# Two-tile sums and products of a decoder trunk moved from GpSimd to VectorE

## The chip, the core and the metric

The kernel runs on one core of one Trainium2 chip. The core has five engines with an instruction queue each: TensorE (PE in the profile; its weight loads are PEld), VectorE (DVE), ScalarE (ACT), GpSimd (POOL) and SyncE (SP, which here only issues DMAs). Each engine works its queue in order; semaphores tie the queues together. The metric is the device time of one execution in microseconds (us); lower is better.

## The reference

A decoder trunk of two layers over 1024 tokens of width 1024, in float32. Layer 0 has a mixer of differential attention (4 heads, two softmax maps each) beside causal pooling (4 groups of 128 channels, trailing means over 2, 4, 8 and 16 tokens minus the token itself); layer 1 has a gated short convolution. After the mixer each layer has cross-attention into 256 memory tokens and a squared-ReLU MLP of width 4096. Each sub-layer is preceded by an RMSNorm and followed by a residual addition.

```python
def even_mixer(h, w_in, w_out, ...):
    ...
    o = diff_attention(q1, q2, k1, k2, v, lam, bias_dist)
    o = rms_norm(o, subln_g) * (1.0 - lambda_init)
    y = multi_scale_pool(u, pool_w, pool_scale)      # windows 2, 4, 8, 16
    return jnp.concatenate([o, y], axis=-1) @ w_out

def odd_mixer(h, w_in, conv_w, w_out):
    z = c_gate * x_part                              # three parts of h @ w_in
    y = conv3(z, conv_w)                             # causal, 3 taps
    return (b_gate * y) @ w_out

def reference(x, mem, ...):
    h = x
    for l in range(2):
        h = h + (even_mixer if l % 2 == 0 else odd_mixer)(rms_norm(h, ...), ...)
        h = h + cross_attention(rms_norm(h, ...), mem_n, wq, wkv, wo)
        a = jax.nn.relu(rms_norm(h, ...) @ w1)
        h = h + (a * a) @ w2
    return rms_norm(h, final_norm_g)
```

## The kernel before

Activations lie channel-major: a tile is 128 channels by 1024 tokens, and an activation of width 1024 is eight such tiles. Every matrix product is computed three times in a fast format of TensorE: `cut` splits a float32 tile into a high part (written by ACT, L72 or L75) and a low part (the rest, a subtraction on DVE, L73 or L76), and PE adds high by high, low by high and high by low in PSUM.

**Weights.** `order` lists all weight blocks in the sequence of their use. `w_load` starts their DMAs on SP into raw buffers `wr` (four of them), `w_cut` cuts one block into `wh` and `wl` (two each). The products with wq, w1 and w2 use a scheme of seven block products instead of eight (`split_gemm`, matmuls on L277). Its weights come in pair units of two raws `a` and `b` (72 units). A unit gives four weight blocks: `a`, the sum tile `wt`, the changed `a`, and half of `b`. Four sums of 128x512 make them: L149 and L150 write the two halves of `wt`, L152 and L153 change `a` after it has been cut. L135 to L139 are the same for the last unit. Before, these sums run on POOL.

**Products.** `split_gemm` runs its seven steps over three PSUM banks (`_x` and the two halves of `_yz`). After each step `out` evacuates a bank with raised priority: L1021 (ACT), L1023 and L1025 (DVE) in the MLP's first product (tiles `m0a`, `m1a`), L1095 (DVE) in its second (`m0b`, `m1b`), L912 in the query product of the cross-attention (`c0q`, `c1q`). A step that writes a bank waits until the bank has been evacuated.

**MLP.** `up(p)` runs 16 rounds per layer; behind each, `squares` applies scale, ReLU and square (L1010 on DVE, L1011 on ACT), `combine` forms operand sums on DVE (L259 to L262), and `store` sends the round's result to DRAM. The second product has 4 chunks of 4 steps; `fetch` and `ready` bring the stored tiles back and cut them (`m1A_...`), for the next chunk while this one runs.

**Norms.** `Norm.add` adds the squares of a tile: ACT squares it into `sq` (L323) and POOL adds it into `acc` (L324; in four places with `last=True` DVE does it). `stage1` sums over channels with PE transposes (L332) and a DVE reduction (L333), and takes the power on POOL (L336); `stage2` spreads the result with PE again (L345).

**Attention and pooling.** In the first 400 us products for the four heads and four pooling groups fill PE between the steps of the softmax chains (L579 and L580 on DVE, L581 on ACT, L590, L591, L593 on DVE, transposes L612 and products L628 on PE). `fill_u(g)` computes the channels `u` of a pooling group and then a chain of doubling sums: g+1 levels of shift-and-add, a correction of the first columns, scaling, and the subtraction of `u`. Before, all of it stands on POOL right behind `u` (L518 to L526), and the cut of the result follows as `window` some program steps later: `soon(n, fn)` runs `fn` after `n` further steps.

**Order.** The loop over `k` at the start (cuts of the input `x` and of the first weights `w0p`, squares of `x`, and the first products `q0ps`, `k0ps` on L415) stands under a manual schedule: each engine takes its instructions in the order in which they are written. The rest is placed by the language's scheduler by priority and its own estimate of durations, so that instructions moved to another engine also move their neighbours. The convolution, `conv_mixer`, multiplies twice on POOL per tile (L1148, L1155).

Of the kernel before, what the change touches and what calls it, by code (L numbers as in the profile page):

```python
# [13 lines left out]
AF = mybir.ActivationFunctionType  # L14
# [26 lines left out]
def hybrid_trunk(ctx: ExitStack, tc: tile.TileContext, xT, memT, vecs, lams, rel, onehot, negrow, invcnt,  # L41
# [21 lines left out]
    def f32(t):  # L63
        return t.bitcast(F32)
# [53 lines left out]
    def w_cut():  # L118
        u, g = state["unit"], state["group"]
        if u >= len(order):  # L120
            return
        shape = list(order[u][0])
        raw = raws[u]
        hi = sb.tile(shape, F32R, tag="wh", bufs=2, name=f"wh{u}_{g}")
        lo = sb.tile(shape, F32R, tag="wl", bufs=2, name=f"wl{u}_{g}")
        done = False
        if len(raw) == 1:
            cut(hi, lo, raw[0])
            done = True
        else:  # L130
            a, b = raw[0], raw[1]
            if g == 0 and u in tails:
                t = sb.tile(shape, F32, tag="wt", bufs=1, name=f"wt{u}")
                raw.append(t)
                nc.gpsimd.tensor_add(t[:, 4:], b[:, :4], b[:, 4:])  # L135
                nc.gpsimd.tensor_sub(t[:, :4], b[:, :4], a[:, :4])
                nc.gpsimd.tensor_sub(b[:, :4], a[:, :4], t[:, 4:])
                cut(hi, lo, a)
                nc.gpsimd.tensor_add(a[:, 4:], a[:, 4:], b[:, :4])  # L139
            elif u in tails:  # L140
                if g < 3:
                    cut(hi, lo, raw[g])
                else:
                    cut(hi[:, :4], lo[:, :4], a[:, 4:])
                    done = True
            elif g == 0:
                t = sb.tile(shape, F32, tag="wt", bufs=1, name=f"wt{u}")
                raw.append(t)
                nc.gpsimd.tensor_add(t[:, 4:], b[:, :4], b[:, 4:])  # L149
                nc.gpsimd.tensor_sub(t[:, :4], a[:, :4], t[:, 4:])  # L150
                cut(hi, lo, a)
                nc.gpsimd.tensor_sub(a[:, :4], b[:, :4], a[:, :4])  # L152
                nc.gpsimd.tensor_add(a[:, 4:], a[:, 4:], t[:, :4])  # L153
            elif g == 1:
                cut(hi, lo, raw[2])
            elif g == 2:
                cut(hi, lo, a)
            else:
                cut(hi[:, :4], lo[:, :4], b[:, 4:])
                done = True  # L160
        cuts.append((hi, lo))
        state["group"] += 1
# [144 lines left out]
    class Norm:  # L307
# [7 lines left out]

        def add(self, src, h=None, last=False):
            cs = slice(0, S) if h is None else half(h)
# [3 lines left out]
            else:  # L321
                acc, sq = self.acc[None], slot(f"{self.name}_sq")
                nc.scalar.activation(sq[:, cs], src, AF.Square)  # L323
                (nc.vector if last else nc.gpsimd).tensor_add(acc[:, cs], acc[:, cs], sq[:, cs])  # L324

# [179 lines left out]
    def fill_u(g):  # L505
# [7 lines left out]
        yield from gemm_halves(X, nm, ev)  # L513
        cur = u
        for lvl in range(g + 1):
            sh = 1 << lvl
            nxt = slot(f"{nm}_s{lvl}")
            nc.gpsimd.tensor_add(nxt[:, sh:], cur[:, sh:], cur[:, : S - sh])  # L518
            nc.gpsimd.tensor_copy(nxt[:, :sh], cur[:, :sh])
            cur = nxt  # L520
        pc = {}

        nc.gpsimd.tensor_mul(cur[:, : w - 1], cur[:, : w - 1], icnt[:, g, : w - 1])
        pl = slot(f"{nm}_p")
        nc.gpsimd.tensor_scalar(cur, cur, 1.0 / w, 1.0, op0=ALU.mult, op1=ALU.mult)
        nc.gpsimd.tensor_sub(pl, cur, u)  # L526

        def window():
            pc[0], pc[1] = pair(f"{nm}_p")
            nc.scalar.activation(pc[0], pl, AF.Copy)  # L530
            nc.gpsimd.tensor_sub(pc[1], pl, f32(pc[0]))
            soon(8, tail)
# [9 lines left out]

        soon(10 + 7 * (g + 1), window)

# [285 lines left out]
    def residual(act, g_col, name, split=False):  # L830
# [4 lines left out]
        for n in range(KT):  # L835
# [10 lines left out]
            if split and n == KT - 1:  # L846
                w, ps = w_next(), psg(f"{name}_{n}")
                for h in range(2):
# [152 lines left out]
    def mlp(l, X, nrm, g_next, name):  # L1001
# [78 lines left out]
        for c in range(4):  # L1080
            for p in range(KT // 2):
# [53 lines left out]
    def conv_mixer(X, nrm, g_next, name):  # L1135
        hooks = with_norm(nrm)
        Y = Halves()
        for j in range(KT):
# [122 lines left out]
```

## Time and profile before

| | |
|---|---|
| time, median of 3 runs | 2588.26 us (2587.04 to 2589.97) |
| the profiled execution | 2590.47 us, of which 2588.7 us are the span of its instructions |
| granted TensorE clock, mean | 0.993 |
| busy: PE, DVE, ACT, POOL | 2513.6, 1739.8, 1069.1, 729.2 us |
| instructions on DVE and POOL in the profile | 1972, 439 |

The span is the time from the first to the last instruction of the profiled execution, and its rows are in microseconds from its start. A row of the timeline gives start, duration, engine, line, operation, output and inputs; in square brackets stands how long the engine had waited and for whom. Neighbouring rows of one form are merged with a count. The row's duration is longer than the distance to the next start, since neighbours overlap a little at their ends.

### The profile page before, as it was taken

How to read it: one execution, taken by the hardware profiler on the slowest of the kernel's cores; microseconds unless marked ns; L12 is line 12 of the kernel's file. 1: busy time of each engine (PE TensorE's matmuls, PEld its weight loads, DVE VectorE, ACT ScalarE, POOL GpSimd, SP SyncE). 2: the span in 40 equal slices, each digit the busy share in tenths (PEclk: the TensorE clock that was granted, in tenths of full speed). 3: DMA queues.
4: the chain of work that ended last, by engine and by line, in shares of the span. 5: the costliest groups of instructions: out<-in, count | busy, mean ns of one | idle time of the engine just before them, and what ended most of it. 6: DMA issues, size and time to landing. Idle time of an engine off the chain costs nothing. (4 is left out here: it accounts for less than half of the span.)

```text
span 2588.7 us, 30102 instructions
## 1 busy us (share of the span) xinstructions
PE 2513.6 (97%) x11522; PEld 2053.3 (79%) x11522; DVE 1739.8 (67%) x1972; ACT 1069.1 (41%) x1503; POOL 729.2 (28%) x439
## 2 busy tenths in 40 slices
PE   7999999999999999999999999999999999999997
PEld 5777778888878888777888888878887888777786
DVE  7767764756577778877773333575567777877875
ACT  4554564445443344433342111344544334433432
POOL 3222200330224334323352111231033334322334
PEclk9999999999999999999999999999999999999999
DMA  5101146221324436776732111322133444776752
GB/s 172 33 25 42 57 155 211 106 76 64 123 94 142 170 136 224 280 272 246 258 139 73 49 49 50 138 79 92 49 122 114 156 157 159 264 272 242 267 204 92
DMA packets 108432, 365.91 MB, mean 141 GB/s; under 512 B 12416, under 2 KB 14848, under 8 KB 108288
## 3 DMA queue, kind: packets, MB, share of 16 engines
q1 hardware_dynamic: 74880, 252.82, 28.8%
q10 hardware_dynamic: 33408, 111.16, 11.3%
q8 instruction: 91, 1.49, 0.2%
q14 instruction: 53, 0.43, 0.1%
HBM read 249.91 MB, written 114.03 MB: 141 GB/s over the span
## 5 line engine op out<-in xcount | busy, mean ns | idle before, releaser
L72 ACT ACTIVATE wh<-wr 128x1024 fp32r<-128x1024 f32 (+1 forms) x318 | 305.9, 962 | 806.8 <-PE m0b_yz L277 147.2
L73 DVE TENSOR_TENSOR wl<-wr,wh 128x1024 fp32r<-128x1024 f32 (+1 forms) x318 | 365.9, 1151 | 109.9 <-ACT wh L72 109.7
L152 POOL TENSOR_TENSOR wr<-wr,wr 128x512 f32<-128x512 f32 x71 | 104.4, 1470 | 762.8 <-DVE wl L73 758.6
L73 DVE TENSOR_TENSOR wl<-wt,wh 128x1024 fp32r<-128x1024 f32 x72 | 148.4, 2062 | 7.3 <-ACT wh L72 7.1
L153 POOL TENSOR_TENSOR wr<-wr,wt 128x512 f32<-128x512 f32 x71 | 142.0, 2000 | 0.0
L150 POOL TENSOR_TENSOR wt<-wr,wt 128x512 f32<-128x512 f32 x71 | 135.5, 1909 | 5.3
L149 POOL TENSOR_TENSOR wt<-wr 128x512 f32<-128x512 f32 x71 | 101.4, 1428 | 122.7 <-issue 75.0
L72 ACT ACTIVATE wh<-wt 128x1024 fp32r<-128x1024 f32 x72 | 75.9, 1055 | 62.7 <-PE m1b_x L277 18.7
L1148 POOL TENSOR_TENSOR cv_z<-cv_z,cv_cg 128x1024 f32<-128x1024 f32 x8 | 26.2, 3275 | 175.4 <-DVE cv_z L1147 175.4
L201 PE MATMUL X<-Y,wh 128*128 128x512 f32 x256 | 69.8, 390 | 0.0
L581 ACT ACTIVATE s_p<-s,s_negm 128x128 f32<-128x128 f32 (+7 forms) x64 | 47.2, 739 | 29.1 <-DVE s_negm L580 26.1
L201 PEld LDWEIGHTS X<-Y,wh 128*128 128x128 f32 x256 | 48.0, 188 | 10.2 <-DVE X1h L851 0.3
L1010 DVE SCALAR_TENSOR_TENSOR m0a_r<-m0a_r,c0o_rbc 128x1024 f32<-128x1024 f32 x32 | 52.8, 1656 | 0.9
L1010 DVE SCALAR_TENSOR_TENSOR m1a_r<-m1a_r,c1o_rbc 128x1024 f32<-128x1024 f32 x32 | 52.8, 1656 | 0.9
L1011 ACT ACTIVATE m1a_r<-m1a_r 128x1024 f32<-128x1024 f32 x32 | 34.0, 1062 | 43.3 <-DVE m1a_r L1010 43.3
L1011 ACT ACTIVATE m0a_r<-m0a_r 128x1024 f32<-128x1024 f32 x32 | 34.0, 1062 | 43.3 <-DVE m0a_r L1010 43.3
L324 POOL TENSOR_TENSOR c1o_acc<-c1o_acc,c1o_sq 128x1024 f32<-128x1024 f32 x6 | 15.5, 2588 | 119.5 <-ACT c1o_sq L323 119.5
L324 POOL TENSOR_TENSOR c0o_acc<-c0o_acc,c0o_sq 128x1024 f32<-128x1024 f32 x6 | 15.5, 2589 | 118.6 <-ACT c0o_sq L323 118.6
L1025 DVE TENSOR_TENSOR m1a_r<-m1a_r,m1a_yz 128x512 f32<-128x512 f32 x32 | 22.0, 686 | 36.9 <-PE m1a_yz L277 36.4
L1025 DVE TENSOR_TENSOR m0a_r<-m0a_r,m0a_yz 128x512 f32<-128x512 f32 x32 | 22.0, 686 | 36.9 <-PE m0a_yz L277 36.4
L580 DVE TENSOR_REDUCE s_negm<-s 128x1 f32<-128x128 f32 (+7 forms) x64 | 46.4, 748 | 0.2
L324 POOL TENSOR_TENSOR X_acc<-X_acc,X_sq 128x1024 f32<-128x1024 f32 x6 | 15.5, 2587 | 92.7 <-ACT X_sq L323 92.7
(2695 smaller groups left out, 7999.2 us busy)
## 6 DMA issues: line engine op xcount, KB each, us to landing
wr<-in_w_dram SPq DMA_DIRECT2D x128, 512.0 KB, 3.9
m0f<-m0a_d SPq DMA_DIRECT2D x48, 512.0 KB, 6.1
m1f<-m1a_d SPq DMA_DIRECT2D x48, 512.0 KB, 5.9
wr<-in_wkv_dram SPq DMA_DIRECT2D x32, 512.0 KB, 3.6
m0a_d<-m0a_r ACTq DMA_DIRECT2D x32, 512.0 KB, 2.8
m1a_d<-m1a_r ACTq DMA_DIRECT2D x32, 512.0 KB, 2.9
wr<-in_conv_in_dram SPq DMA_DIRECT2D x24, 512.0 KB, 3.6
wr<-in_wq_dram SPq DMA_DIRECT2D x16, 512.0 KB, 3.7
```

The lines of the kernel that those rows point to most:

```text
L72: nc.scalar.activation(hi, src, AF.Copy)
L73: nc.vector.tensor_sub(lo, src, f32(hi))
L149: nc.gpsimd.tensor_add(t[:, 4:], b[:, :4], b[:, 4:])
L150: nc.gpsimd.tensor_sub(t[:, :4], a[:, :4], t[:, 4:])
L152: nc.gpsimd.tensor_sub(a[:, :4], b[:, :4], a[:, :4])
L153: nc.gpsimd.tensor_add(a[:, 4:], a[:, 4:], t[:, :4])
L201: nc.tensor.matmul(ps, wt[:, k, :], act.part(k, i, h), start=(k == 0 and wt is hi and i == 0), stop=(k == ks - 1 and wt is lo))
L324: (nc.vector if last else nc.gpsimd).tensor_add(acc[:, cs], acc[:, cs], sq[:, cs])
L580: nc.vector.tensor_reduce(s["negm"][:, m : m + 1], ps[:, :L], axis=AX.X, op=ALU.max, negate=True)
L581: nc.scalar.activation(s["pr"][m][:, :L], ps[:, :L], AF.Exp, bias=s["negm"][:, m : m + 1], accum_out=s["den"][:, m : m + 1])
L1010: nc.vector.scalar_tensor_tensor(v, v, 0.0, b(), op0=ALU.max, op1=ALU.mult)
L1011: nc.scalar.activation(t, t, AF.Square)
```

## The change

All two-tile sums and products of the weight units, the norms, the pooling and the convolution are issued on DVE instead of POOL. `Norm.add` loses its argument `last`. The pooling is also rewritten: the levels of the doubling sum are no longer issued in one piece behind `u`, but dealt over later program steps by `soon(4 + 6 * lvl, ...)`; ACT copies the first columns of a level (L521 after), the correction stays a product (L526), scaling and subtraction become one instruction (L527), and the result's low part is cut by `cut`. On POOL remain the powers (L336, L723), the zero fills (L617), the products of the last norm (L1173) and set-up: 61 instructions instead of 427. DVE has 2301 instead of 1932.

```diff
@@ w_cut: weight sums of a pair unit (the last unit likewise) @@
             elif g == 0:
...
-                nc.gpsimd.tensor_add(t[:, 4:], b[:, :4], b[:, 4:])
-                nc.gpsimd.tensor_sub(t[:, :4], a[:, :4], t[:, 4:])
+                nc.vector.tensor_add(t[:, 4:], b[:, :4], b[:, 4:])
+                nc.vector.tensor_sub(t[:, :4], a[:, :4], t[:, 4:])
                 cut(hi, lo, a)
-                nc.gpsimd.tensor_sub(a[:, :4], b[:, :4], a[:, :4])
-                nc.gpsimd.tensor_add(a[:, 4:], a[:, 4:], t[:, :4])
+                nc.vector.tensor_sub(a[:, :4], b[:, :4], a[:, :4])
+                nc.vector.tensor_add(a[:, 4:], a[:, 4:], t[:, :4])
@@ Norm.add @@
-                (nc.vector if last else nc.gpsimd).tensor_add(acc[:, cs], acc[:, cs], sq[:, cs])
+                nc.vector.tensor_add(acc[:, cs], acc[:, cs], sq[:, cs])
@@ fill_u @@
-        cur = u
-        for lvl in range(g + 1):
+        cur = {0: u}
+        pc = {}
+
+        def level(lvl):
             sh = 1 << lvl
             nxt = slot(f"{nm}_s{lvl}")
-            nc.gpsimd.tensor_add(nxt[:, sh:], cur[:, sh:], cur[:, : S - sh])
-            nc.gpsimd.tensor_copy(nxt[:, :sh], cur[:, :sh])
-            cur = nxt
-        pc = {}
-
-        nc.gpsimd.tensor_mul(cur[:, : w - 1], cur[:, : w - 1], icnt[:, g, : w - 1])
-        pl = slot(f"{nm}_p")
-        nc.gpsimd.tensor_scalar(cur, cur, 1.0 / w, 1.0, op0=ALU.mult, op1=ALU.mult)
-        nc.gpsimd.tensor_sub(pl, cur, u)
+            nc.vector.tensor_add(nxt[:, sh:], cur[lvl][:, sh:], cur[lvl][:, : S - sh])
+            nc.scalar.activation(nxt[:, :sh], cur[lvl][:, :sh], AF.Copy)
+            cur[lvl + 1] = nxt
 
         def window():
+            c, pl = cur[g + 1], slot(f"{nm}_p")
+            nc.vector.tensor_mul(c[:, : w - 1], c[:, : w - 1], icnt[:, g, : w - 1])
+            nc.vector.scalar_tensor_tensor(pl, c, 1.0 / w, u, op0=ALU.mult, op1=ALU.subtract)
             pc[0], pc[1] = pair(f"{nm}_p")
-            nc.scalar.activation(pc[0], pl, AF.Copy)
-            nc.gpsimd.tensor_sub(pc[1], pl, f32(pc[0]))
+            cut(pc[0], pc[1], pl)
             soon(8, tail)
...
-        soon(10 + 7 * (g + 1), window)
+        for lvl in range(g + 1):
+            soon(4 + 6 * lvl, lambda lvl=lvl: level(lvl))
+        soon(4 + 6 * (g + 1), window)
@@ conv_mixer @@
-            nc.gpsimd.tensor_mul(z, z, cg)
+            nc.vector.tensor_mul(z, z, cg)
...
-            nc.gpsimd.tensor_mul(y, y, nrm.rbc)
+            nc.vector.tensor_mul(y, y, nrm.rbc)
```

At the start, in the loop over `k`, the squares' additions now stand in DVE's own queue, behind the cut of the same input tile. The piece of the difference on DVE (a row is line, operation, output and inputs with the tile's size):

```order
 L73 TENSOR_TENSOR w0p0l<-w_0_92,w0p0h 128x256
 L76 SCALAR_TENSOR_TENSOR X1l<-x_85,vec,X1h 128x1024
+L324 TENSOR_TENSOR n_acc<-n_acc,n_sq 128x1024
 L73 TENSOR_TENSOR w0p0l<-w_0_92,w0p0h 128x256
 L76 SCALAR_TENSOR_TENSOR X2l<-x_86,vec,X2h 128x1024
+L324 TENSOR_TENSOR n_acc<-n_acc,n_sq 128x1024
 L73 TENSOR_TENSOR w0p0l<-w_0_92,w0p0h 128x256
 L76 SCALAR_TENSOR_TENSOR X3l<-x_87,vec,X3h 128x1024
+L324 TENSOR_TENSOR n_acc<-n_acc,n_sq 128x1024
```

One addition of 128x1024 has come between the cut of an input tile and that of the next weight block, in each of seven turns.

In the second product of layer 1's MLP, where its second chunk begins (tile `m1b1h`), DVE's rows before:

```order
L73 TENSOR_TENSOR wl_1_17674<-wt_17635,wh_1_17673 128x1024
L1095 TENSOR_TENSOR m1b1h_17528<-m1b1h_17528,m1b_0_x 128x512
L73 TENSOR_TENSOR m1A_2_0l<-m1f_2_0_17595,m1A_2_0h 128x1024
L73 TENSOR_TENSOR m1A_2_1l<-m1f_2_1_17597,m1A_2_1h 128x1024
L1095 TENSOR_TENSOR m1b1h_17528<-m1b1h_17528,m1b_0_yz 128x512
L73 TENSOR_TENSOR wl_2_17716<-wr_0_17449,wh_2_17715 128x1024
```

The same place in the changed kernel, on DVE:

```order
L152 TENSOR_TENSOR wr_0_17445<-wr_1_17447,wr_0_17445 128x512
L153 TENSOR_TENSOR wr_0_17445<-wr_0_17445,wt_17631 128x512
L1095 TENSOR_TENSOR m1b0h_17388<-m1b0h_17388,m1b_3_x 128x512
L73 TENSOR_TENSOR m1A_1_3l<-m1f_1_3_17555,m1A_1_3h 128x1024
L73 TENSOR_TENSOR wl_1_17670<-wt_17631,wh_1_17669 128x1024
L1095 TENSOR_TENSOR m1b1h_17524<-m1b1h_17524,m1b_0_x 128x512
L149 TENSOR_TENSOR wt_17805<-wr_1_17589 128x512
L73 TENSOR_TENSOR m1A_2_0l<-m1f_2_0_17591,m1A_2_0h 128x1024
L1095 TENSOR_TENSOR m1b1h_17524<-m1b1h_17524,m1b_0_yz 128x512
L73 TENSOR_TENSOR m1A_2_1l<-m1f_2_1_17593,m1A_2_1h 128x1024
L73 TENSOR_TENSOR wl_2_17712<-wr_0_17445,wh_2_17711 128x1024
```

Ahead of the evacuation of the `yz` bank stood two cuts of 128x1024; now one sum of 128x512 and one cut stand there. The same rows stand at the start of the three later chunks of both layers.

In a round of the MLP's first product (layer 1), DVE's rows before, from the copy L1023 on:

```order
L1023 COPY m1a_r_15753<-m1a_x 128x512
L1010 SCALAR_TENSOR_TENSOR m1a_r_15753<-m1a_r_15753,c1o_rbc 128x1024
L73 TENSOR_TENSOR wl_1_15896<-wt_15871,wh_1_15895 128x1024
L1025 TENSOR_TENSOR m1a_r_15891<-m1a_r_15891,m1a_yz 128x512
L73 TENSOR_TENSOR wl_2_15928<-wr_0_15693,wh_2_15927 128x1024
```

And in the changed kernel, on DVE:

```order
L1023 COPY m1a_r_15749<-m1a_x 128x512
L152 TENSOR_TENSOR wr_0_15689<-wr_1_15691,wr_0_15689 128x512
L153 TENSOR_TENSOR wr_0_15689<-wr_0_15689,wt_15867 128x512
L73 TENSOR_TENSOR wl_1_15892<-wt_15867,wh_1_15891 128x1024
L1010 SCALAR_TENSOR_TENSOR m1a_r_15749<-m1a_r_15749,c1o_rbc 128x1024
L149 TENSOR_TENSOR wt_16005<-wr_1_15829 128x512
L150 TENSOR_TENSOR wt_16005<-wr_0_15827,wt_16005 128x512
L1025 TENSOR_TENSOR m1a_r_15887<-m1a_r_15887,m1a_yz 128x512
L73 TENSOR_TENSOR wl_2_15924<-wr_0_15689,wh_2_15923 128x1024
```

The four sums of a unit stand between the copy and the evacuation of `yz`, and the second product L1010 has moved behind the cut of `wl_1`. On ACT the evacuation L1021 of `m1a_x` stood behind the square L1011 that needs this L1010; in the changed kernel it stands ahead of it.

More of the change, by code (lines that the diff above doesn't have):

```diff
@@ L134, in w_cut @@
                 raw.append(t)
-                nc.gpsimd.tensor_add(t[:, 4:], b[:, :4], b[:, 4:])
-                nc.gpsimd.tensor_sub(t[:, :4], b[:, :4], a[:, :4])
-                nc.gpsimd.tensor_sub(b[:, :4], a[:, :4], t[:, 4:])
+                nc.vector.tensor_add(t[:, 4:], b[:, :4], b[:, 4:])
+                nc.vector.tensor_sub(t[:, :4], b[:, :4], a[:, :4])
+                nc.vector.tensor_sub(b[:, :4], a[:, :4], t[:, 4:])
                 cut(hi, lo, a)
-                nc.gpsimd.tensor_add(a[:, 4:], a[:, 4:], b[:, :4])
+                nc.vector.tensor_add(a[:, 4:], a[:, 4:], b[:, :4])
             elif u in tails:
@@ L148, in w_cut @@
                 raw.append(t)
-                nc.gpsimd.tensor_add(t[:, 4:], b[:, :4], b[:, 4:])
-                nc.gpsimd.tensor_sub(t[:, :4], a[:, :4], t[:, 4:])
+                nc.vector.tensor_add(t[:, 4:], b[:, :4], b[:, 4:])
+                nc.vector.tensor_sub(t[:, :4], a[:, :4], t[:, 4:])
                 cut(hi, lo, a)
-                nc.gpsimd.tensor_sub(a[:, :4], b[:, :4], a[:, :4])
-                nc.gpsimd.tensor_add(a[:, 4:], a[:, 4:], t[:, :4])
+                nc.vector.tensor_sub(a[:, :4], b[:, :4], a[:, :4])
+                nc.vector.tensor_add(a[:, 4:], a[:, 4:], t[:, :4])
             elif g == 1:
@@ L314, in __init__, with add @@
             self.rbc = None
-        def add(self, src, h=None, last=False):
+        def add(self, src, h=None):
             cs = slice(0, S) if h is None else half(h)
@@ L854, in residual @@
                         nx.group(0, j, r[0])
-                        nn.add(t[:, half(h)], h, last=True)
+                        nn.add(t[:, half(h)], h)
                     else:
@@ L876, in residual @@
             if split and n == KT - 1:
-                nx.late = {2: [lambda: nx.group(2, j, r[1])], 3: [lambda: nn.add(t[:, half(1)], 1, last=True)],
+                nx.late = {2: [lambda: nx.group(2, j, r[1])], 3: [lambda: nn.add(t[:, half(1)], 1)],
                            4: [lambda: nx.group(3, j, t4[:, :H]), lambda: h_store(n, t, name)]}
@@ L1090, in squares_of @@
                 def squares_of(n, h):
-                    return lambda: nn.add(t[n][:, half(h)], h, last=True)
+                    return lambda: nn.add(t[n][:, half(h)], h)
                 def evac(n, h, ps, new):
```

## Prediction

> **What bounds the kernel now.** I read the engines' busy shares first, then the groups by shape, then who PE waits for, then the timeline at each of those waits.
>
> ```profile
> PE 2513.6 (97%) x11522; PEld 2053.3 (79%) x11522; DVE 1739.8 (67%) x1972; ACT 1069.1 (41%) x1503; POOL 729.2 (28%) x439
> ```
>
> PE is the bound; nothing can be won but the 75 us of the span (2588.7 less 2513.6) in which it is not busy, and matmuls at half clock. The profiled execution took 2590.47 us, 2.2 above the median of 2588.26. The question is how much of the 75 us is DVE's lateness, and why DVE, busy two thirds of the time, is late.
>
> ```profile
> L73 DVE TENSOR_TENSOR wl<-wr,wh 128x1024 fp32r<-128x1024 f32 x246 | 314.0, 1276 | 61.7 <-ACT wh L72 61.6
> L73 DVE TENSOR_TENSOR wl<-wt,wh 128x1024 fp32r<-128x1024 f32 x72 | 148.4, 2062 | 7.3 <-ACT wh L72 7.1
> L1010 DVE SCALAR_TENSOR_TENSOR m1a_r<-m1a_r,c1o_rbc 128x1024 f32<-128x1024 f32 x32 | 52.8, 1656 | 0.9
> L259 DVE TENSOR_TENSOR m1a_t<-m1a_r,m1a_r 128x512 f32<-128x512 f32 x16 | 25.2, 1576 | 0.0
> L262 DVE TENSOR_TENSOR m1a_t<-m1a_r,m1a_t 128x512 f32<-128x512 f32 x16 | 10.9, 683 | 0.0
> L149 POOL TENSOR_TENSOR wt<-wr 128x512 f32<-128x512 f32 x71 | 101.4, 1428 | 122.7 <-issue 75.0 <-DMA wr<-in_wq_dram 20.8 <-DMA wr<-in_w_dram 20.3
> ```
>
> Same engine, same shape, different means: a cut of 128x1024 takes 1.28 us from `wr` and 2.06 from `wt`, a sum of 128x512 takes 0.68 on L262 and 1.58 on L259. The long ones are those that run while POOL works. At the start:
>
> ```profile
> 11.54 20.11 POOL L324 TENSOR_TENSOR n_acc<-n_acc,n_sq 128x1024 f32<-128x1024 f32 x7 [10.23 <-ACT n_sq L323]
> 14.29 3.39 DVE L76 SCALAR_TENSOR_TENSOR X2l<-x,vec,X2h 128x1024 fp32r<-128x1024 f32 x1
> 17.61 2.62 DVE L73 TENSOR_TENSOR w0p0l<-w,w0p0h 128x256 fp32r<-128x256 f32 x1
> 33.05 0.41 DVE L73 TENSOR_TENSOR w0p1l<-w,w0p1h 128x256 fp32r<-128x256 f32 x1
> 36.05 1.27 DVE L76 SCALAR_TENSOR_TENSOR X7l<-x,vec,X7h 128x1024 fp32r<-128x1024 f32 x1
> 17.74 0.73 PE L415 MATMUL q0ps<-X2l,w0p0h 128*128 128x512 f32 x2 [2.84 <-DVE X2l L76]
> 24.08 1.14 ACT L75 ACTIVATE X7h<-x,vec 128x1024 fp32r<-128x1024 f32 x1
> 41.66 1.29 DVE L333 TENSOR_REDUCE n_ms<-n_n 128x4 f32<-128x512 f32 x2 [2.00 <-PE n_n L332]
> ```
>
> Until POOL's seven additions end at 31.65, `X2l` takes 3.39 us and a cut of 128x256 2.62; behind that end the same forms take 1.27 and 0.41. So the work taken from POOL also gives DVE time back.
>
> **The load.** A moved sum of 128x512 costs DVE 0.61 to 0.68 us (L262's mean, with and without the overlap of neighbours), one of 128x1024 about 1.2 (X7l's 1.27 less an overlap). 288 weight sums give 176 to 196 us; some 80 instructions of squares, convolution and pooling give about 90. Given back are 72 x (2.06 - 1.2), 64 x (1.66 - 1.2) and 32 x (1.58 - 0.68), 120 us from three kinds of row, and more from the others. DVE's busy time rises by at most 170 us, to 74% of the span; I expect it within 60 us of the old value. What decides is where the new work stands in DVE's queue, which is worked in order.
>
> **Start.** DVE's turn of the loop is 3.4 + 2.6 = 6 us now. In the changed order it is 0.41 + 1.27 + 1.2 less overlaps, 2.7 us; PE's own work per turn, twelve matmuls at 0.227 us from start to start (2342.07 to 2342.30 below), is 2.7 too. ACT is no brake: it had `X7h` by 25.2. From 11.8 (the start of `X2l` less one cut's 2.5), six turns and a last cut end `X7l` near 29.3 instead of 37.3, the last square sum follows by 30.5, and PE finishes the transposes that L333 waits for near 32 instead of 41.6. Gain 9.5 us; bounds 8 (`X7l` alone) and 10.
>
> **Attention.** Two places where the pooling chain on POOL delays DVE and, through it, PE:
>
> ```profile
> 215.53 2.75 POOL L518 TENSOR_TENSOR u_s<-u_s 128x1022 f32<-128x1022 f32 x1
> 213.65 2.89 DVE L73 TENSOR_TENSOR wl<-wr,wh 128x1024 fp32r<-128x1024 f32 x1 [0.16 <-ACT wh L72]
> 216.46 2.11 DVE L593 SCALAR_TENSOR_TENSOR s_p<-s_p,rden,s_p 128x256 f32<-128x256 f32 x1
> 219.22 0.69 PE L612 MATMUL tp<-ident,s_p 128*128 128x128 f32 x2 [3.32 <-DVE sub_ms L333]
> ...
> 218.00:225.00 7.00, 5.78 (x16) 4.66 (x17) 3.96 (x9) 1.73 (x5) 6.13 (x8) 0.51 0.54 212
> ...
> 295.06 3.48 POOL L526 TENSOR_TENSOR u_p<-u_s,u_u 128x1024 f32<-128x1024 f32 x1
> 296.25 2.58 DVE L593 SCALAR_TENSOR_TENSOR s_p<-s_p,rden,s_p 128x256 f32<-128x256 f32 x1
> 298.98 0.41 PE L612 MATMUL tp<-ident,s_p 128*128 128x128 f32 x2 [1.86 <-DVE s_p L593]
> 299.90:303.40 3.50, 3.50 (x9) 2.10 (x7) 2.32 (x5) 1.77 (x4) 0.45 (x1) 0.51 0.08 8
> ```
>
> The rows with a colon are stretches: busy time of PE, PEld, DVE, ACT, POOL, then the granted clock. At the free durations of their shapes (1.27 and 0.41) the cut and L593 would be 3.3 us shorter together; I take 2.7 of PE's 3.32 us, because L333 still stands behind them, and 1.8 of the 1.86 at the second place. Behind both stalls the granted clock is a half, 0.51, while PE is busy 5.78 and 3.50 us; half of that, 2.9 and 1.75 us, goes if the stalls go. Together 9.1; bounds 4.5 (stalls alone) and 9.8. The page "TensorE: Matmul & The Clock Gate" of the Trainium skill (Part 1, "What's actually happening") has the clock fall after a whole idle window of about 3.4 us. The rows here show it fall behind waits of 3.32 and 1.86 us, so here the measurement decides; by the page's rule these two half-clock stretches would have another cause and stay, and the sum below would be 4.6 us smaller.
>
> Against it stand 22 pooling instructions of about 1.2 us, 26 us of new work in DVE's queue between softmax steps. I charge 5 us, between 0 (all of it in DVE's idle third) and 13 (half of it ahead of a step that PE waits for). It is nearer to the low end, as in the changed order no two of these levels stand next to each other on DVE.
>
> **The MLP's second product.**
>
> ```profile
> 2340.20 2.16 POOL L150 TENSOR_TENSOR wt<-wr,wt 128x512 f32<-128x512 f32 x1
> ...
> 2339.22 1.98 DVE L73 TENSOR_TENSOR m1A_0l<-m1f,m1A_0h 128x1024 fp32r<-128x1024 f32 x1
> 2341.13 2.32 DVE L73 TENSOR_TENSOR m1A_1l<-m1f,m1A_1h 128x1024 fp32r<-128x1024 f32 x1
> 2343.37 0.67 DVE L1095 TENSOR_TENSOR m1b1h<-m1b1h,m1b_yz 128x512 f32<-128x512 f32 x1
> ...
> 2342.07 0.39 PE L277 MATMUL m1b_x<-m1A_3l,wh 128*128 128x512 f32 x1
> 2342.30 0.39 PE L277 MATMUL m1b_x<-m1A_3h,wl 128*128 128x512 f32 x1
> 2344.10 0.50 PE L277 MATMUL m1b_yz<-m1A_0h,wh 128*128 128x512 f32 x1 [1.42 <-DVE m1b1h L1095]
> ...
> PE m0b_yz L277 <- DVE m0b1h L1095: 1.9, 2, 1.4
> PE m1b_yz L277 <- DVE m1b3h L1095: 1.4, 1, 1.4
> ...
> 2258.94 0.47 PE L277 MATMUL m1b_x<-m1A_0h,wh 128*128 128x512 f32 x1 [1.47 <-DVE m1b0h L1095]
> 2282.56 0.47 PE L277 MATMUL m1b_x<-m1A_0h,wh 128*128 128x512 f32 x1 [1.67 <-DVE m1b0h L1095]
> 2250.00:2300.00 50.00, 44.23 (x187) 34.29 (x187) 44.93 (x45) 23.04 (x26) 17.31 (x11) 1.00 0.79 293
> ```
>
> Two cuts, lengthened to 4.1 us beside POOL's sums (L150 is shown), stand ahead of the evacuation that PE waits 1.4 us for. The list of waits has six such groups (three later chunks in two layers; first and last shown), each with one wait of 1.4. In the changed order the evacuation follows one sum (0.61) and one cut (1.2): from 2339.2 it starts at 2341.0 and ends 0.6 us before PE's last matmul of the step ahead. 6 x 1.4 = 8.4 us; bounds 3 (the wait shrinks to its half, the rest shows up at the next weight cut) and 8.4.
>
> The first chunk is the tightest stretch: in 2250 to 2300 DVE is busy 44.93 of 50 us. The 11 POOL instructions there are 6.7 us more for DVE; its rows there that are longer than their shapes' free time hold, by my estimate from the means above, about as much. I take 3 us gained per layer, the two waits of 1.47 and 1.67, 6 in all; bounds: 6 and minus 3 (6.7 us come, nothing is given back: 1.6 us over 50 per layer). The page "Perfetto Trace Analysis" of the Trainium skill ("Optimizing Scalar/DVE Operations") says that work of a saturated DVE may go to ScalarE or even GpSimd, and speaks here against the change; by it the sum would be 9 us smaller. The other half of its advice, that a move between DVE and GpSimd may not help because they share a port, is the lengthening seen above and speaks for it.
>
> For new waits elsewhere in this product I charge 3 us (0 to 6).
>
> **Transitions, MLP's first product, convolution.**
>
> ```profile
> 1948.23 0.68 DVE L1025 TENSOR_TENSOR m1a_r<-m1a_r,m1a_yz 128x512 f32<-128x512 f32 x1
> 1948.96 0.50 PE L277 MATMUL m1a_yz<-c1o_x_0h,wh 128*128 128x512 f32 x1 [1.55 <-DVE m1a_r L1025]
> 2026.46 0.69 DVE L1025 TENSOR_TENSOR m1a_r<-m1a_r,m1a_yz 128x512 f32<-128x512 f32 x1 [0.47 <-PE m1a_yz L277]
> 1300.00:1720.00 420.00, 420.00 (x1862) 347.76 (x1862) 194.21 (x183) 114.58 (x130) 112.03 (x46) 1.00 0.25 84
> ```
>
> At the four starts of a split product the evacuation comes 0.5 us earlier: 2 us (0 to 6). In a round of the first product four sums (2.45 us) now stand ahead of L1025; L1010 and the cut from `wt` give back 0.45 and 0.85, 0.47 was idle, so it comes 0.7 us later. Its bank is written again a step later, 2.7 us: nothing, and if that cover were gone 0.7 x 32 rounds = 22 us. Convolution: 16 products of 1.2 us lie in DVE's 226 idle us of that stretch, in which PE never stops: nothing.
>
> **The sum.** -9.5 - 9.1 + 5 - 8.4 - 6 + 3 - 2 = -27 us. Against the profiled execution 2563.5, against the median 2561.
>
> **The rivals.**
> The product's waits only move: DVE in 2250 to 2300 is full with or without the change, and the sums now stand before the same evacuations. Then -9.5 - 9.1 + 5 = -14 remains: 2575. For it speaks the 44.93; against it, that the changed order puts less ahead of the evacuation, not more.
> The half clock stays: -27 + 4.6, 2566. For it, 1.86 us is a short wait to cause it; against, that it begins directly behind both.
> No difference: a wait behind each removed one, 2588 within 5 us (0.2%, about what a measurement of this kernel can tell from no change). Against it stands the start, where nothing else is near.
> Slower: L149 waits for its raw. In its row above POOL waited 41 us for DMA, at two products of each layer. On POOL nobody stood behind it; on DVE the evacuations do. All of it on PE's path would give -27 + 41, 2602; it turns to a loss from 27 us on, 7 at each of four places. Against it: DVE is at other work for most of these waits.
>
> **How the numbers follow.** Forecast 0.53 (own range 2548 to 2572), half clock stays 0.10, waits only move 0.20, no difference 0.06, slower 0.08, more gain than forecast 0.03. The range 2547 to 2580 leaves out the slower, the unchanged and little else. Faster 0.86, within 0.2% 0.06, slower 0.08.
>
> **What would show it.** X2l at 1.3 us, L333 for `n_ms` near 32; the wait for `sub_ms` below 1 us and clock 1.00 behind it; no 1.4 us waits for `yz` at the chunks' starts; the mean of `wl<-wt` near 1.2. It is wrong if cuts stay long without POOL, if L1025 in the rounds makes PE wait, or if DVE waits for DMA at L149.

## The result: 35 us faster

The changed kernel takes 2554.11 us (median of 4 runs, 2553.65 to 2555.26) against 2589.06 for the kernel before beside it: a ratio of 0.9867 (95% interval 0.985 to 0.9884), 35 us less. The profiled execution took 2555.26 us, its span is 2553.5. The forecast was 2561, 27 us less.

The busy shares of the changed kernel, from its page:

```profile
PE 2507.3 (98%) x11522; PEld 2055.9 (81%) x11522; DVE 1763.6 (69%) x2341; ACT 1073.2 (42%) x1513; POOL 31.5 (1%) x56
```

DVE took over 369 instructions and is busy only 24 us longer. The groups by shape show why:

```profile
L73 DVE TENSOR_TENSOR wl<-wr,wh 128x1024 fp32r<-128x1024 f32 x246 | 300.3, 1221 | 56.0 <-ACT wh L72 52.7
L73 DVE TENSOR_TENSOR wl<-wt,wh 128x1024 fp32r<-128x1024 f32 x72 | 87.6, 1217 | 0.9 <-ACT wh L72 0.9
L1010 DVE SCALAR_TENSOR_TENSOR m1a_r<-m1a_r,c1o_rbc 128x1024 f32<-128x1024 f32 x32 | 38.9, 1219 | 0.5
L259 DVE TENSOR_TENSOR m1a_t<-m1a_r,m1a_r 128x512 f32<-128x512 f32 x16 | 10.9, 684 | 0.0
L153 DVE TENSOR_TENSOR wr<-wr,wt 128x512 f32<-128x512 f32 x71 | 48.5, 683 | 0.0
L149 DVE TENSOR_TENSOR wt<-wr 128x512 f32<-128x512 f32 x71 | 48.6, 685 | 6.9 <-DMA wr<-in_wq_dram 3.4 <-DMA wr<-in_w_dram 2.9
```

A cut from `wt` fell from 2062 to 1217 ns, L1010 from 1656 to 1219, L259 from 1576 to 684; a weight sum costs DVE 0.68 us. The last row holds the rival "slower": POOL waited 41 us for raws, DVE waits 6.3.

Where the time came from, by the start of a stage's first matmul in the two timelines (us):

| first matmul of | before | after | difference | gained in the stage ahead |
|---|---|---|---|---|
| first norm (`n_n`) | 41.02 | 31.23 | -9.79 | start: 9.8 |
| mixer's output product (`X`) | 420.99 | 407.38 | -13.61 | attention and pooling: 3.8 |
| layer 0's second MLP product (`m0b_x`) | 1043.15 | 1030.66 | -12.49 | output product, cross-attention, first product: -1.1 (lost) |
| convolution (`cv0c`) | 1364.19 | 1340.48 | -23.71 | second product: 11.2 |
| layer 1's second MLP product (`m1b_x`) | 2250.28 | 2225.89 | -24.39 | convolution to first product: 0.7 |
| last norm (`m1b_n`) | 2567.96 | 2532.75 | -35.21 | second product: 10.8 |

The places of the prediction in the changed kernel's timeline, first the start and the first place in the attention:

```profile
13.03 1.28 DVE L76 SCALAR_TENSOR_TENSOR X2l<-x,vec,X2h 128x1024 fp32r<-128x1024 f32 x1
14.23 1.22 DVE L324 TENSOR_TENSOR n_acc<-n_acc,n_sq 128x1024 f32<-128x1024 f32 x1
27.50 1.27 DVE L76 SCALAR_TENSOR_TENSOR X7l<-x,vec,X7h 128x1024 fp32r<-128x1024 f32 x1
32.17 1.28 DVE L333 TENSOR_REDUCE n_ms<-n_n 128x4 f32<-128x512 f32 x2
...
202.49 1.23 DVE L73 TENSOR_TENSOR wl<-wr,wh 128x1024 fp32r<-128x1024 f32 x1
203.63 0.48 DVE L593 SCALAR_TENSOR_TENSOR s_p<-s_p,rden,s_p 128x256 f32<-128x256 f32 x1
204.77 0.44 PE L612 MATMUL tp<-ident,s_p 128*128 128x128 f32 x2
205.00:225.00 20.00, 20.00 (x111) 15.66 (x110) 17.84 (x34) 12.16 (x26) 1.93 (x3) 1.00 0.08 26
```

`X2l` takes 1.28 us and L333 starts at 32.17 instead of 41.66. The wait of 3.32 us for `sub_ms` is gone, and PE is busy for the whole 20 us behind it at clock 1.00.

Then the second place in the attention, a later chunk of the second product, and the new waits (the first of them at the start of the query product, then those in the last round of the MLP's first product and in the first chunk of its second):

```profile
296.36 0.66 PE L612 MATMUL tp<-ident,s_p 128*128 128x128 f32 x4 [1.63 <-ACT sub_rbc L347]
300.00:306.00 6.00, 6.00 (x19) 4.28 (x19) 2.24 (x5) 0.83 (x1) 0.00 (x0) 0.50 0.29 87
...
2311.27 0.68 DVE L149 TENSOR_TENSOR wt<-wr 128x512 f32<-128x512 f32 x1
2311.87 1.22 DVE L73 TENSOR_TENSOR m1A_0l<-m1f,m1A_0h 128x1024 fp32r<-128x1024 f32 x1
2313.00 0.68 DVE L1095 TENSOR_TENSOR m1b1h<-m1b1h,m1b_yz 128x512 f32<-128x512 f32 x1
2270.00:2530.00 260.00, 260.00 (x1148) 215.28 (x1147) 203.23 (x255) 99.98 (x109) 0.00 (x0) 1.00 0.62 217
...
501.43 0.50 PE L277 MATMUL c0q_x<-X_x_0h,wh 128*128 128x512 f32 x1 [0.96 <-ACT c0q_r L910]
1012.39 0.50 PE L277 MATMUL m0a_x<-c0o_x_0h,wl 128*128 128x512 f32 x1 [1.28 <-DVE wl L73]
1037.68 0.50 PE L277 MATMUL m0b_yz<-m0A_0h,wh 128*128 128x512 f32 x1 [0.88 <-DVE m0b0h L1095]
1044.56 0.50 PE L277 MATMUL m0b_x<-m0A_0l,wh 128*128 128x512 f32 x1 [0.57 <-DVE m0A_0l L73]
1030.00:1052.00 22.00, 18.85 (x77) 13.60 (x76) 21.92 (x27) 14.43 (x17) 0.00 (x0) 1.00 0.67 246
```

At the second place another releaser (ACT) now ends a wait of 1.63 us, and the half clock still follows. By the trace's record of the clock it lasts from 298.13 to 308.37 us, 10.24 us; in the kernel before it lasted 6.83 us at the first place and 3.41 at the second, 10.24 as well. In the later chunks the evacuation comes 1.7 us behind the sum, and from 2270 to 2530 PE never stops. New are a wait of 0.96 us for ACT at the start of each split product (four in all, in place of waits of 1.55 us for DVE's evacuation) and one of 1.28 us in the last round of each first product. In the first chunk DVE is busy 21.92 of 22 us, and PE waits several times for less than a microsecond.

### The profile page after: what moved, and what is told of

Its sections match the earlier page's. It is cut to its first block, busy times and chain, and to the rows that moved or that the text cites. A ratio compares the mean times of both kernels' runs of the same rounds, so it can differ in the third digit from the quotient of the medians.

```text
span 2553.5 us, 29777 instructions
## 1 busy us (share of the span) xinstructions
PE 2507.3 (98%) x11522; PEld 2055.9 (81%) x11522; DVE 1763.6 (69%) x2341; ACT 1073.2 (42%) x1513; POOL 31.5 (1%) x56
## 4 chain that ended last, share of the span: by engine, by line
PE 93%; DVE 3%; DMA 1%; ACT 1%; issue 1%; SPq 0%; POOL 0%; DVEq 0%; ACTq 0%
PE m0a_x L277 7%; PE m1a_x L277 7%; PE m0b_x L277 7%; PE m1b_x L277 7%; PE m0a_yz L277 5%; PE m1a_yz L277 5%; PE m1b_yz L277 5%; PE m0b_yz L277 5%; PE qkv L201 4%; PE cvo L201 3%; PE X L201 3%; PE c0o L201 3%; PE c1o L201 3%; PE kv_ps L744 3%; PE c1q_x L277 2%; PE c0q_x L277 2%
## 5 line engine op out<-in xcount | busy, mean ns | idle before, releaser
L73 DVE TENSOR_TENSOR wl<-wt,wh 128x1024 fp32r<-128x1024 f32 x72 | 87.6, 1217 | 0.9 <-ACT wh L72 0.9
L149 DVE TENSOR_TENSOR wt<-wr 128x512 f32<-128x512 f32 x71 | 48.6, 685 | 6.9 <-DMA wr<-in_wq_dram 3.4
L150 DVE TENSOR_TENSOR wt<-wr,wt 128x512 f32<-128x512 f32 x71 | 48.8, 688 | 1.3
L152 DVE TENSOR_TENSOR wr<-wr,wr 128x512 f32<-128x512 f32 x71 | 48.7, 686 | 1.0
L153 DVE TENSOR_TENSOR wr<-wr,wt 128x512 f32<-128x512 f32 x71 | 48.5, 683 | 0.0
L1011 ACT ACTIVATE m0a_r<-m0a_r 128x1024 f32<-128x1024 f32 x32 | 34.0, 1063 | 31.9 <-DVE m0a_r L1010 31.7
L1011 ACT ACTIVATE m1a_r<-m1a_r 128x1024 f32<-128x1024 f32 x32 | 34.0, 1062 | 31.8 <-DVE m1a_r L1010 31.7
L1025 DVE TENSOR_TENSOR m1a_r<-m1a_r,m1a_yz 128x512 f32<-128x512 f32 x32 | 21.9, 684 | 31.3 <-PE m1a_yz L277 31.1
L1025 DVE TENSOR_TENSOR m0a_r<-m0a_r,m0a_yz 128x512 f32<-128x512 f32 x32 | 21.9, 684 | 31.3 <-PE m0a_yz L277 31.1
L1021 ACT ACTIVATE m1a_r<-m1a_x 128x512 f32<-128x512 f32 x32 | 19.1, 598 | 56.0 <-PE m1a_x L277 54.2
L1021 ACT ACTIVATE m0a_r<-m0a_x 128x512 f32<-128x512 f32 x32 | 19.1, 598 | 56.0 <-PE m0a_x L277 54.1
L201 PE MATMUL X<-Y,wl 128*128 128x512 f32 x128 | 40.7, 389 | 0.0
L277 PE MATMUL m0b_x<-m0A,wh 128*128 128x512 f32 x128 | 39.5, 390 | 0.7 <-DVE m0b0h L1095 0.7
L277 PE MATMUL m1a_x<-c1o_x,wh 128*128 128x512 f32 x128 | 39.5, 390 | 0.0
L277 PE MATMUL m0a_x<-c0o_x,wh 128*128 128x512 f32 x128 | 39.5, 390 | 0.0
```

The costliest lines, as they stand in the source:

```text
L73: nc.vector.tensor_sub(lo, src, f32(hi))
L149: nc.vector.tensor_add(t[:, 4:], b[:, :4], b[:, 4:])
L150: nc.vector.tensor_sub(t[:, :4], a[:, :4], t[:, 4:])
L152: nc.vector.tensor_sub(a[:, :4], b[:, :4], a[:, :4])
L153: nc.vector.tensor_add(a[:, 4:], a[:, 4:], t[:, :4])
L201: nc.tensor.matmul(ps, wt[:, k, :], act.part(k, i, h), start=(k == 0 and wt is hi and i == 0), stop=(k == ks - 1 and wt is lo))
```

## Experiments

Theory A: POOL's two-tile instructions on SBUF lengthen DVE's, and the gain is the end of that. Theory B: the gain comes from another order of the instructions or from the placing of the sums. The kernel before took 2588.8 to 2589.3 us beside these kernels.

**One part at a time.** Four kernels each move one part of the change and leave the rest as before.

```diff
# start: only the first norm's square sums
-        n0.add(xs[k])
+        n0.add(xs[k], last=True)
# weights: only the sums in w_cut (all eight lines)
-                nc.gpsimd.tensor_add(t[:, 4:], b[:, :4], b[:, 4:])
+                nc.vector.tensor_add(t[:, 4:], b[:, :4], b[:, 4:])
# pooling: fill_u as in the change
# norms and convolution: square sums of all other norms, and
-            nc.gpsimd.tensor_mul(z, z, cg)
+            nc.vector.tensor_mul(z, z, cg)
```

> The kernel before, with only the seven square sums of the first norm (L324, n_acc) moved to DVE. Theory A (POOL's reads of SBUF lengthen DVE's two-tile instructions, and the gain comes stage by stage from ending that): X2l takes 1.3 us instead of 3.4, the first norm's transposes start near 31.3 us instead of 41.0, and nothing behind them takes it back: 9.8 us less than before, 2579. Theory B (the gain comes from the new order of the whole program, or later waits absorb a shift of the start): below 5 us.

> The kernel before, with only the 288 weight sums on DVE. Theory A: the MLP's second products each lose the 11 us that they lost in the full change, the starts of the split products lose some 0.2 each, the last round of each first product may get the new wait of 1.4 us: 19 to 23 us less than before, 2566 to 2570. Theory B (the sums alone crowd DVE's queue, and the gain there needs the squares moved as well): below 10 us, or slower.

> The kernel before, with only the pooling rewritten and moved to DVE. Theory A: the stretch up to the output projection of the mixer loses the 3.8 us that it lost in the full change behind the start: 2 to 5 us less than before, 2584 to 2587. Theory B (what the stretch won came from the shift of 9.8 us against the DMA stream, not from the pooling): within 1.5 us of before.

> The kernel before, with the square sums of all norms but the first and the convolution's products on DVE. PE waits for nothing in the convolution and next to nothing in the output products where these sums lie. Theory A: no difference, within 2 us of before. Theory B (the square sums of the MLP's last chunk are part of the 11 us won in each second product): 3 us or more less than before.

Measured: start 2578.41 us (ratio 0.9963, 0.995 to 0.9977), 10.4 less. Weights 2576.18 (0.995, 0.9938 to 0.9963), 12.6 less. Pooling 2585.54 (0.9988, 0.9979 to 0.9997), 3.2 less. Norms and convolution 2593.6 (1.0016, 1.0008 to 1.0025), 4.8 more.

The start and the pooling came out as theory A said. In the profile of the pooling kernel the first norm stands where it stood before and the mixer's output product starts 5.4 us earlier, so the pooling's gain there does not need the shift of the start. The weights fell between the theories (19 to 23 us were expected by A, below 10 by B), and for the norms neither theory held: they cost time alone. Together the four make 21.4 us, the full change 35.

Most of what the norms cost lies at the starts of the four split products. ACT's rows there, first in the kernel before, then in the kernel with norms and convolution, and PE's wait behind them:

```profile
513.21 0.60 ACT L910 ACTIVATE c0q_r<-c0q_x 128x512 f32<-128x512 f32 x1
513.71 1.05 ACT L72 ACTIVATE wh<-wr 128x1024 fp32r<-128x1024 f32 x1
...
513.64 1.06 ACT L72 ACTIVATE wh<-wr 128x1024 fp32r<-128x1024 f32 x1
514.60 0.58 ACT L910 ACTIVATE c0q_r<-c0q_x 128x512 f32<-128x512 f32 x1
515.23 0.50 PE L277 MATMUL c0q_x<-X_x_0h,wh 128*128 128x512 f32 x1 [1.02 <-ACT c0q_r L910]
```

The scheduler has put the cut of a weight block on ACT ahead of the evacuation that PE needs. PE waits 1.0 us for it in `c0q_x`, `m0a_x`, `c1q_x` and `m1a_x`, and the old waits for DVE there stay (1.4 us each). The weights-only kernel and the full change have the same four waits for ACT, but not the old ones. So the order of the instructions does cost time here; it works against the change.

In the weights-only kernel the second products gained 4.9 and 8.4 us instead of 11.2 and 10.8. Its timeline in layer 0's last chunk shows where a part of the rest was lost:

```profile
1320.81 2.64 POOL L324 TENSOR_TENSOR m0b_acc<-m0b_acc,m0b_sq 128x1024 f32<-128x1024 f32 x1 [10.28 <-ACT m0b_sq L323]
1326.23 2.46 POOL L324 TENSOR_TENSOR m0b_acc<-m0b_acc,m0b_sq 128x1024 f32<-128x1024 f32 x1 [2.79 <-ACT m0b_sq L323]
1321.11 3.42 DVE L73 TENSOR_TENSOR wl<-wt,wh 128x1024 fp32r<-128x1024 f32 x1
1326.38 3.41 DVE L76 SCALAR_TENSOR_TENSOR m0b_x3l<-m0b3h,vec,m0b_x3h 128x1024 fp32r<-128x1024 f32 x1
1329.71 0.68 DVE L1095 TENSOR_TENSOR m0b3h<-m0b3h,m0b_yz 128x512 f32<-128x512 f32 x1
1330.44 0.50 PE L277 MATMUL m0b_yz<-m0A_0h,wh 128*128 128x512 f32 x1 [2.16 <-DVE m0b3h L1095]
```

The square sums left on POOL meet a DVE that now carries the weight sums as well. POOL's addition ends at 1323.45, and the cut that began at 1321.11 ends 1.08 us later, at 1324.53: nearly all of its work, 1.22 us without POOL, seems to have been done behind POOL's end. With `m0b_x3l` it is the same, and PE waits 2.16 us for the evacuation behind it, a wait that neither the kernel before nor the full change has.

**Pairs of parts.** Two kernels test that reading: the full change with the weight sums back on POOL, and weights, norms and convolution together without start and pooling.

```diff
# the changed kernel, all but weights (eight lines)
-                nc.vector.tensor_add(t[:, 4:], b[:, :4], b[:, 4:])
+                nc.gpsimd.tensor_add(t[:, 4:], b[:, :4], b[:, 4:])
# the kernel before with weights, norms and convolution: w_cut and the convolution as in the change, and
-                (nc.vector if last else nc.gpsimd).tensor_add(acc[:, cs], acc[:, cs], sq[:, cs])
+                (nc.gpsimd if self.name == "n0" else nc.vector).tensor_add(acc[:, cs], acc[:, cs], sq[:, cs])
```

> The changed kernel with the weight sums back on POOL. If the parts simply add, the single parts (start -10.3, pooling -3.2, norms and convolution +4.8) give 8.7 us less than before, 2580. If the parts help one another beyond that (less POOL work in the same stretch), 2 us or more below 2578; if DVE's fuller queue meets POOL's sums, above 2582.

> The kernel before with weight sums, convolution and all square sums but the first norm's on DVE; start and pooling as before. The single parts add to -12.6 + 4.8 = -7.8 us, 2581. If the 3 us square sums on POOL are what made new waits in the weights-only kernel (last chunk of layer 0, 1323 to 1347 us), both parts together lose the 11.2 and 10.8 us of the second products that the full change lost: 20 to 24 us less than before, 2565 to 2569.

Measured: all but weights 2579.53 us (0.9964, 0.995 to 0.9977), 9.5 less than before, near the plain sum of 8.7. Weights, norms and convolution together 2565.36 (0.991, 0.9897 to 0.9924), 23.7 less, where the single parts add to 7.8. The second products gained 10.3 and 10.8 us in it. So the norms cost 4.8 us while POOL forms the weight sums and bring 11.1 once it doesn't; the weight sums bring 12.6 alone and 25.4 as the last part. About 8 us of this interaction lie in the second products (13.2 us gained there by the weights alone, nothing by the norms alone, 21.1 by both): there two kinds of POOL work meet in the same stretches. Some 4 us are the waits for ACT, which each of the two single kernels has and which stand only once in the kernel with both. The rest is not located, and part of it can be the clock: up to the mixer's output product PE, DVE and ACT run the same instructions in the same order in the profiles of both kernels, yet that product starts at 423.40 us with the weights alone and at 417.43 with both.

**POOL's work given back, with the order held.** Two kernels add useless POOL work to the changed kernel, four instructions per pair unit. The rows of PE and DVE stand in the same order as in the changed kernel, and DVE waits for none of the added instructions.

```diff
# reads: behind L150, and behind L153 with a in place of t, twice each
+                nc.gpsimd.tensor_add(scr, t[:, :3], t[:, 4:7])
# writes: at the same places, twice each, behind a copy of one column on ACT
+                nc.gpsimd.memset(scr, 0.0)
```

> The changed kernel with extra work that nothing uses: per pair unit four sums of 128x384 on POOL that read two halves of wt (two, behind L150) or of the changed raw (two, behind L153). PE's and DVE's instructions stand in the same order as in the changed kernel. Theory A (POOL's reads of SBUF lengthen DVE's two-tile instructions): DVE's cuts from wt go from 1.22 us towards 2, the MLP's second products lose their waits' gain again and more, as DVE now also carries its own sums: 15 to 45 us more than the changed kernel, 2569 to 2599. Theory B (the order of the instructions and the placing of the sums make the gain): the same as the changed kernel within 3 us, 2551 to 2557.

> The changed kernel with extra work that nothing uses: per pair unit four zero fills of 128x384 on POOL, which only write, paced by two single-column copies on ACT. PE's and DVE's instructions stand in the same order as in the changed kernel. Theory A in its narrow form (POOL's reads through a shared port block, writes do not; so states the Trainium skill, SBUF - State Buffer, Who interferes with whom): DVE's rows keep their 0.68 and 1.22 us, and the time is the changed kernel's within 3 us. Theory A in its wide form (any work of POOL on SBUF lengthens DVE's): 5 us or more above the changed kernel.

Measured: with reads 2586.61 us (0.9993, 0.9984 to 1.0002), which is no different from the kernel before; with writes 2553.98 (0.9865, 0.9852 to 0.9879), the changed kernel's time. From the groups by shape of the kernel with reads:

```profile
PE 2520.0 (98%) x11522; PEld 2050.6 (79%) x11522; DVE 1909.6 (74%) x2341; ACT 1073.4 (42%) x1513; POOL 475.7 (18%) x340
L149 DVE TENSOR_TENSOR wt<-wr 128x512 f32<-128x512 f32 x71 | 83.7, 1179 | 7.5 <-DMA wr<-in_wq_dram 3.2 <-DMA wr<-in_w_dram 2.8
L73 DVE TENSOR_TENSOR wl<-wt,wh 128x1024 fp32r<-128x1024 f32 x72 | 101.9, 1416 | 0.9 <-ACT wh L72 0.9
L1010 DVE SCALAR_TENSOR_TENSOR m1a_r<-m1a_r,c1o_rbc 128x1024 f32<-128x1024 f32 x32 | 50.4, 1577 | 0.5
L259 DVE TENSOR_TENSOR m1a_t<-m1a_r,m1a_r 128x512 f32<-128x512 f32 x16 | 22.6, 1412 | 0.0
```

And of the kernel with writes:

```profile
L73 DVE TENSOR_TENSOR wl<-wt,wh 128x1024 fp32r<-128x1024 f32 x72 | 87.6, 1216 | 0.9 <-ACT wh L72 0.9
L150 POOL MEMSET scr<- 128x384 f32 x142 | 59.6, 419 | 1114.6 <-ACT scr L150 1110.5
```

With the same instructions in the same order, POOL's reads add 146 us to DVE's busy time and 32.5 us to the kernel. The cut from `wt` grew less than I expected (1.42, not near 2): POOL's reads fell on L149, L1010 and L259 instead. As many instructions of POOL that only write leave DVE's rows as they were. They are shorter, 119 us in all against 444; if they lengthened DVE's work as the reads do, DVE's busy time would grow by some 39 us (an estimate: 146 times 119 by 444), and it is 1763.5 us against 1763.6. The kernel with reads keeps its gain at the start (10.5 us in the profile) and in the attention (3.9), where it has no added work, and its second products take 5.8 us more than before instead of 22.0 less. So the order of the instructions does not make the gain there, and the wide form of theory A is out. For the start and the attention POOL's work was not given back; there the one-part kernels and the rows of `X2l` and L593 speak for theory A, and the pooling's rewriting is not separated from its move. The Trainium skill ("SBUF - State Buffer", "Who interferes with whom") says that a DVE instruction with two SBUF inputs contends with a GpSimd instruction that reads SBUF, not with one that only writes: these two kernels agree. It calls the ports that the two share an exclusive lock: the cut of the weights-only kernel that ended 1.08 us behind POOL agrees with that.

**Two tries at the rest.** The first takes a cut out of the way of the new 1.28 us wait; the second also takes DVE work out of the full stretch behind it.

```diff
# both
-                return {1: [fetch(c, 0, (2, 3))], 4: [ready(c, 0, (2,))], 5: [ready(c, 0, (3,))]}
+                return {1: [fetch(c, 0, (2, 3))], 4: [ready(c, 0, (2,))]}
...
-                return {2: [fetch(c, 1)], ...
+                return {1: [ready(c, 0, (3,))], 2: [fetch(c, 1)], ...
# the second only
-        late = {5: rest[1], 6: rest[2]}, {2: rest[3], 4: rest[5]}
+        late = {}, {1: rest[1], 2: rest[2], 3: rest[3], 5: rest[5]}
-                if new and (n, h) != (1, 0):
+                if new and ((n, h) != (1, 0) or p == 2 * KT - 1):
```

> The changed kernel with one cut of 128x1024 (m0A_3l, m1A_3l of the next operand) taken out of DVE's queue ahead of the weight cut that PE waits 1.28 us for in the last round of each first product, and put into the following step. If that wait is DVE's order alone, it goes in both layers: 2 to 3 us less than the changed kernel, 2551 to 2552. If DVE is simply full from there into the second product, the wait comes back in its first chunk: the same as the changed kernel within 1 us.

> As the kernel with the cut moved, and besides in each layer the squares and operand sums of the last round (two L1010 of 1.22 us, four sums) are put off from the first to the second step of the second product, and the copy L1023 of the last round goes to ACT. This takes some 4 us of DVE work out of the stretch of 20 us (1030 to 1052) in which DVE is never idle in the changed kernel and PE waits 0.88, 0.40, 0.57, 0.60 and 0.70 us for it. If DVE's load bounds that stretch, 5 to 8 us less than the changed kernel over both layers, 2546 to 2549; if the work only moves its waits to the second step, 2 to 3 us less, as with the cut alone.

Measured: 2553.15 us (0.9856, 0.9839 to 0.9872) and 2554.96 (0.9866, 0.9851 to 0.988): by their medians neither differs from the changed kernel. In both profiles `m0b_x` starts 1.6 to 1.8 us earlier, and the convolution at the same time as without the edit. The first one's timeline in the first chunk:

```profile
1041.23 0.50 PE L277 MATMUL m0b_x<-m0A_3l,wh 128*128 128x512 f32 x1 [1.81 <-DVE m0A_3l L73]
1040.00:1045.00 5.00, 3.02 (x7) 1.75 (x8) 4.78 (x8) 4.52 (x6) 0.00 (x0) 0.73 0.94 333
1045.00:1052.00 7.00, 6.92 (x22) 5.16 (x20) 5.36 (x8) 3.31 (x7) 0.00 (x0) 0.70 0.94 338
```

The waits of under a microsecond have become one of 1.81, and behind it part of both stretches runs at half clock (0.73 and 0.70), where the changed kernel has 1.00 with its scattered waits. The second kernel has a wait of 1.54 us there, and its mean clock from 1028 to 1052 is 0.93. Its DVE did get free time in that stretch (21.59 of 24 us busy, 23.74 in the changed kernel), so DVE's load over the whole stretch is not what decides; whether its order does was not tested. The expected 5 to 8 us were wrong.

The profile of the first kernel shows its longest execution. The record of the clock has two stretches of 6.83 us at half clock there, one in each layer's first chunk, which the changed kernel has not. Its four executions took 2550.01, 2551.54, 2554.76 and 2555.53 us at mean clocks of 0.994, 0.993, 0.991 and 0.991; the changed kernel's took 2553.65 to 2555.26 at 0.993 to 0.994. So the edit seems to win some 3 to 4 us where the clock stays and to lose them where it falls. No profile of such a shorter execution was taken, so this is not shown.

## Why the prediction held, step by step

**Start**: -9.5 predicted, -9.8 in the profile, -10.4 by itself.

**Attention**: -9.1 + 5 predicted, -3.8 in the profile. The sum is right and the parts are not; that the sum fits is luck. The first place gave all that was expected, stall and clock (5.8 us in 200 to 250). The second gave nothing: a wait of 1.63 us for ACT's `sub_rbc`, one of 0.60 behind it and a longer half clock took the old one's place. Over the whole stretch PE's waits fell from 9.8 to 5.5 us, 4.3 where 4.5 were expected, and the half clock stayed at 10.24 us, where 4.6 us of gain were expected from its end. The 5 us charged for the new work on DVE show in no wait: PE's waits for DVE there fell from 7.9 to 1.4 us. So the step that failed is the half clock, and the charge that was not needed hid it. The pooling kernel takes the same 4.3 us out of PE's waits. That the profile of the full change is only 0.9 us ahead of the start-only kernel at the mixer's output product is the clock: the start-only kernel has 3.41 us of half clock in that stretch, the full change 10.24.

**The MLP's second product**: -8.4 - 6 + 3 predicted, -22.0 measured (11.2 and 10.8). The mechanism was right, the size was off: 10.6 us more than forecast, which is more than the 8 us by which the whole forecast fell short. The first chunks gained 2.9 and 3.0 us, as forecast, though other waits (0.88, 0.40, 0.57, 0.60 and 0.70 us) stand there now. Two terms were mis-sized. The 8.4 for the later chunks measured 16.1 (8.3 and 7.8 us by the starts of the chunks): the waits of 1.4 us went, and so did those below 1 us, which I left out of the sum; together they were 6.4 and 5.7 us before and none are left. The remaining 4 us of the 16.1 are not in PE's idle time. The +3 for new waits in the later chunks measured 0. The saturated stretch, on which the rule of the Trainium skill ("Perfetto Trace Analysis", "Optimizing Scalar/DVE Operations") spoke against the change, did stay full (21.92 of 22 us), but gained.

**Transitions and first product**: -2 predicted, 0.4 us lost by the table. The four waits of 1.55 us for DVE went, more than forecast, but the four for ACT (0.96) came, about 0.6 us gained at each start; the new wait in the last round of both first products (2.6 us together) offset that. I had followed DVE's queue there and not ACT's, whose order changed too. In the steady rounds L1025 still waits for PE, as predicted. **Convolution**: 0 predicted, 0 measured, in the full change and alone.

**The rivals.** "Slower" by DVE's waits for raws: 6.3 us of waits instead of 41, nothing on PE's path that shows. "Waits only move" was wrong for the change; the two tries behind it gained nothing in the median, one wait there giving way to another. "Half clock stays" was right for the clock and wrong for the time: in the profiles it left the first place and lasts three times as long at the second, 10.24 us in all as before. "No difference" is out by the start alone.

## What to carry to other kernels

Two engines that read SBUF two tiles at a time are not two engines: before moving work to GpSimd to unload VectorE, compare the same shape's duration on VectorE beside GpSimd's work and without it. Move all of such work from a stretch or none: a part that is left behind meets a fuller queue, and here the weight sums moved alone won 13.2 us in the second products, and 21.1 with the square sums. When instructions move, look at every engine's new order, not only at the two that trade work: four waits of 1 us for ACT came with this change, and an order without them is still to be tried (an estimate from these rows: up to 4 us). Where one engine is full for a whole stretch, a wait that is taken away can come back as another, and several short waits can be better than one long one if the clock follows the long one.

## What the runs showed of the hardware

The half clock is not a fixed price of a wait. In the start-only kernel the same wait for `sub_ms` stands as in the kernel before, with the same two lengthened instructions (2.89 and 2.10 us) ahead of it, and the clock stayed:

```profile
206.45 2.10 DVE L593 SCALAR_TENSOR_TENSOR s_p<-s_p,rden,s_p 128x256 f32<-128x256 f32 x1
205.00:215.00 10.00, 6.68 (x30) 4.61 (x29) 8.35 (x15) 2.99 (x8) 9.05 (x9) 1.00 0.45 158
```

So it took 2.6 us less through the attention than the kernel before, beyond its own shift. In the trace's record of the clock, the half clock of the two places begins in the kernel before at 218.04 and 299.96 us, 81.92 apart, which is 24 times 3.413; it lasts two times 3.413 at the first and once at the second. That fits the free-running window of 3.4 us in the Trainium skill ("TensorE: Matmul & The Clock Gate", Part 1, "What's actually happening"), and with it that one wait can fall across two windows or into one. Counted in such steps from the edges that the record shows, the wait of the kernel before has 2.1 us in the window that ends at 218.04; in the start-only kernel (half clock from 286.01, so an edge at 207.50) the same wait is parted into 1.6 and 1.7 us. That a whole idle window is needed doesn't agree: waits of 1.86 and 1.81 us sufficed here.

How the windows lie differs from execution to execution: the weights-only kernel and the one with weights, norms and convolution run the same instructions as the kernel before up to the mixer's output product, and in the three profiles half clock takes 20.5, 6.8 and 13.7 us of that stretch, and the product starts at 423.40, 417.43 and 420.99 us. A difference of 3 us between two single profiles of this kernel can be the clock alone.
